# Low parts of the weights made by adding transfers instead of VectorE subtractions, in the first projection of a decoder trunk

## The chip, the cores and the metric

The kernel runs on one core of a Trainium2 chip. What is measured is the device time of one execution in microseconds. Engines are named as in the profile: PE is TensorE (matrix products; PEld its weight loads), DVE is VectorE, ACT is ScalarE, POOL is GpSimd, and SP is SyncE, which here only issues transfers.

## The reference

One recurrent layer (RG-LRU) is followed by one attention layer, on a sequence of 1024 positions with 1024 channels. The change lies in the first projection of the recurrent layer:

```python
h = rms_norm(x, norm_g)
u = h @ w_in                                  # 1024 x 1024 times 1024 x 2560
xb, gate = u[..., :D_RNN], u[..., D_RNN:]     # D_RNN = 1280
xb = causal_depthwise_conv(xb, conv_w, conv_b)
r = sigmoid(einsum(xblk, w_rg) + b_rg)        # 10 blocks of 128 channels
i = sigmoid(einsum(xblk, w_ig) + b_ig)
a = exp(log_a);  bterm = sqrt(-expm1(2 log_a)) * (i * xb)
y = scan(a, bterm) * silu(gate);  x = x + y @ w_out
```

## The kernel before

All arrays lie with channels on the 128 partitions and positions along the row. Products are made in a rounded 32-bit type (`F32R`) in three passes, to keep nearly the full precision of float32: each factor is split into a high part (rounded) and a low part (what the rounding left), and `mm3` (L116 to L119) adds high times high (L117), high times low (L118) and low times high (L119). The weight is the first factor, so L119 is the only one of the three that reads the low part of the weights, `wl`; L117 and L118 read the high part, `wh`.

Weights come in blocks of 128 rows by 512 columns (256 KB), two blocks for one output tile of 128 channels (`wtile`, `wload`). For each block, SP loads the raw values into `wr`. In the form used for most blocks of the first projection (`cast=True`), POOL's queue issues a second transfer of the same bytes that rounds them on the way into `wh` (L100), and VectorE subtracts `wh` from `wr` and writes `wl` (L101). The other form (`hl`, L85 and L86) rounds on ScalarE and subtracts on VectorE. There are two buffers for `wr`, four for `wh` and four for `wl`, so the blocks of two output tiles are held at once, and a buffer is written again when TensorE has read it for the last time.

The stage begins with column tile 0, whose weights come in the `hl` form while x is loaded and split. Its products run over eight pieces of x. Meanwhile the squares of x are summed in `accp`; the sum is split (`t`, L85 and L86), added over partitions by products with ones (L362), and turned into the norm's factor on ScalarE and VectorE (L142 to L145). The factor is applied to the products later, so those of tile 1 need not wait for it. Behind the ones-products TensorE goes on with the convolution branch of tile 1, whose two blocks are the first of the `cast` form; their low parts are `wl_327` and, in the order below, `wl_333` before and `wl_334` after.

Then a loop runs over ten column tiles. In each, TensorE makes 48 products of 128x512 for the gate half, 48 for the convolution half of the next tile and 12 for the two gates `r` and `i`. ScalarE and VectorE do the convolution (L382, L384), the sigmoids, the exponentials and roots, and the scan. The nine later gate blocks (`wgate`, 128 KB, one buffer) are of the `cast` form too. That makes 36 blocks of 256 KB and nine of 128 KB.

Each engine works through its own list in order. The lists come from a scheduler that goes by priorities and by its own estimates; the start of the stage, on SP, ScalarE and VectorE, is kept in the order in which it is written. POOL's queue is a list too: a transfer that waits holds up those behind it.

Of the kernel before, what the change touches and what calls it, by code (L numbers as in the profile page):

```python
# [11 lines left out]
AF = mybir.ActivationFunctionType  # L12
ALU = mybir.AluOpType
# [47 lines left out]
def trunk(tc, xT, wina, vecs, wgate, wouta, winc, wuk, wuv, wuq, wuqr, woutb, rope, outT):  # L61
    nc = tc.nc
    V, A, T, G = nc.vector, nc.scalar, nc.tensor, nc.gpsimd
# [10 lines left out]
    def nm(s):  # L74
        uid[0] += 1
        return f"{s}_{uid[0]}"
# [4 lines left out]
    def f(ap):  # L81
        return ap.bitcast(F32)

    def hl(src, hi, lo):
        A.activation(out=hi, in_=src, func=AF.Copy)  # L85
        V.tensor_tensor(out=lo, in0=src, in1=f(hi), op=ALU.subtract)  # L86

    def wload(src, n, gain=None, tag="w", pool=wp, rb=2, hb=4, pri=True, cast=False):

        with tc.high_priority(offset=WPRI if pri else 0):  # L90
            raw = pool.tile([P, n], F32, tag=tag + "r", bufs=rb, name=nm("wr"))
            hi = pool.tile([P, n], F32R, tag=tag + "h", bufs=hb, name=nm("wh"))
            lo = pool.tile([P, n], F32R, tag=tag + "l", bufs=hb, name=nm("wl"))
            nc.sync.dma_start(out=raw, in_=src)
            if gain is not None:
                k = n // P
                r3 = raw.rearrange("p (k m) -> p k m", m=P)
                V.tensor_tensor(out=r3, in0=r3, in1=gain.unsqueeze(2).to_broadcast([P, k, P]), op=ALU.mult)
            if cast:
                G.dma_start(out=hi, in_=src)  # L100
                V.tensor_tensor(out=lo, in0=raw, in1=f(hi), op=ALU.subtract)  # L101
            else:
                hl(raw, hi, lo)
        return hi, lo

    def wtile(src, nk, gain=None, step=4, cast=False, pri=True):

        ks = []
        for k0 in range(0, nk, step):
            k1 = min(nk, k0 + step)  # L110
            hi, lo = wload(src[:, k0 * P:k1 * P], (k1 - k0) * P, None if gain is None else gain[:, k0:k1], cast=cast, pri=pri)
            for k in range(k1 - k0):
                ks.append((hi[:, k * P:(k + 1) * P], lo[:, k * P:(k + 1) * P]))
        return ks
# [175 lines left out]
    with tc.manual_schedule(engines={_E.SP, _E.Activation, _E.DVE}):  # L290
# [60 lines left out]
        for k in range(done, NKT):  # L351
            squares(k)
        ws = wload(wgate[0], 2 * P, tag="s", pool=ta, rb=1, hb=1)
        wx = wtile(wina[1], NKT, cast=True)
        ap = [(tt(F32R), tt(F32R)) for _ in range(2)]
# [87 lines left out]
    for ct in range(NCT):  # L443
        ps = ps0[:2] if ct == 0 else psn
        pg1 = pg1 if ct == 1 else None
        if ct:
            ws = wload(wgate[ct], 2 * P, tag="s", pool=ta, rb=1, hb=1, cast=True)
        if 0 < ct < NCT - 1:
            wx = wtile(wina[ct + 1], NKT, cast=True)
        elif ct:  # L450
            wo = wtile(wouta[0], NCT)
        xcs = conv(ct, ps)
        gt = gates_a(ct, wg, (ps0[2:], pg1, None)[min(ct, 2)])
        if prev is not None:
            tail(*prev)
        if ct + 1 < NCT:
            wg = wtile(wina[NCT + ct + 1], NKT, cast=True)
            psn = [pst(), pst()]
            for h in range(2):
                mmt(psn[h], wx, xs, hs(h))  # L460
            if ct == 0:
                pg1 = [pst(), pst()]
                for h in range(PG1):
                    mmt(pg1[h], wg, xs, hs(h))
            prev = (ct, rgig(ct, ws, xcs), gt)
            if ct == 0:
                for h in range(PG1, 2):
                    mmt(pg1[h], wg, xs, hs(h))
# [129 lines left out]
    for k0, k1 in ((0, 4), (4, 6), (6, 10)):  # L598
        for i in range(2):
            hi, lo = wload(wouta[3 + 4 * i][:, k0 * P:k1 * P], (k1 - k0) * P)  # L600
# [595 lines left out]
```

## Time and profile before

| What | Value |
|---|---|
| median of three runs | 866.79 us (866.57 to 866.79) |
| span of the profiled execution, first to last instruction | 864.5 us |
| TensorE busy | 851.9 us (99%) |
| VectorE busy | 659.5 us (76%) |
| ScalarE busy | 519.9 us (60%) |
| POOL busy | 73.6 us (9%) |
| subtractions of the changed form (L101) | 45, from 28.4 to 244.1 us |
| table loads in ScalarE's list | 45 |
| mean granted TensorE clock | 0.996 |

Times in the profile run from the span's start. A row of the timeline gives start, length, engine, line, operation, `out<-in` and the count of instructions merged; in brackets stands the idle time before it and what ended that. A row of groups gives the count, the busy time with the mean of one in ns, and the idle time before. A row of transfers gives count, size and median time from issue to landing. Neighbouring instructions of one engine overlap a little, so starts are closer together than lengths.

### The profile page before, as it was taken

Reading aid. Unit: us, or ns where it says so; the run is one execution under the profiler, and the core shown is the slowest. Engines: PE = TensorE matmul, PEld = TensorE weight load, DVE = VectorE, ACT = ScalarE, POOL = GpSimd, SP = SyncE. Lnnn points to the kernel's source line nnn. Section 1 sums busy time; section 2 is a strip of 40 time slices with the busy share of each in tenths; the row PEclk is TensorE's granted clock in tenths of the full one; section 3 lists DMA queues with packets and bytes.
Section 4 is the critical chain, followed back from the end, with each engine's and each line's share of the span. In section 5 each row is a group of like instructions: output and inputs, shape, how many; then the busy total and the mean of one; then the engine's idle time right before and its main releaser. Section 6 shows DMA issues by size and latency. Waiting matters only on the chain.

```text
span 864.5 us, 11922 instructions
## 1 busy us (share of the span) xinstructions
PE 851.9 (99%) x4206; PEld 721.7 (83%) x4206; DVE 659.5 (76%) x1216; ACT 519.9 (60%) x959; POOL 73.6 (9%) x143
## 2 busy tenths in 40 slices
PE   8999999999999999999999999999999999999995
PEld 6788888888888888888888889888998998888885
DVE  7888778777877773779998957887797887875254
ACT  8557787777688542699976555555565564431132
POOL 1000110110000110100312320000000000010000
PEclk9999999999999999999999999999999999999998
DMA  8333333333213445123545674122231323867022
GB/s 300 92 98 98 98 97 99 107 95 98 79 43 92 151 144 184 51 98 121 170 147 202 213 252 125 53 91 83 77 113 62 105 82 132 335 211 247 0 98 98
DMA packets 51052, 108.98 MB, mean 126 GB/s; under 512 B 6448, under 2 KB 15024, under 8 KB 50992
## 3 DMA queue, kind: packets, MB, share of 16 engines
q1 hardware_dynamic: 34928, 67.05, 23.7%
q0 software_dynamic: 15216, 40.51, 14.1%
q8 instruction: 33, 0.54, 0.3%
q10 hardware_dynamic: 848, 0.66, 0.2%
q14 instruction: 27, 0.22, 0.1%
HBM read 81.46 MB, written 26.21 MB: 125 GB/s over the span
## 4 chain that ended last, share of the span: by engine, by line
PE 95%; DVE 2%; issue 1%; DMA 1%; ACT 1%; SPq 0%; DVEq 0%
PE ps L118 18%; PE ps L117 18%; PE ps L119 18%; PE pm L119 6%; PE pm L117 6%; PE pm L118 6%; PE pm L922 4%; PE pm L938 2%; PE pm L939 2%; PE s L905 2%; PE s L903 2%; PE s L904 2%; PE s L906 2%; PE s L902 2%; PE pm L937 2%
## 5 line engine op out<-in xcount | busy, mean ns | idle before, releaser
L118 PE MATMUL ps<-pg,wh 128*128 128x512 f32 x664 | 258.7, 390 | 0.6 <-DVE pg L256 0.5
L119 PE MATMUL ps<-pg,wl 128*128 128x512 f32 x664 | 258.4, 389 | 0.0
L117 PE MATMUL ps<-pg,wh 128*128 128x512 f32 x664 | 257.8, 389 | 0.0
L118 PEld LDWEIGHTS ps<-pg,wh 128*128 128x128 f32 x664 | 124.6, 188 | 27.7 <-DVE pg L256 2.1
L117 PEld LDWEIGHTS ps<-pg,wh 128*128 128x128 f32 x664 | 124.6, 188 | 26.3 <-DVE tk L657 0.3
L119 PEld LDWEIGHTS ps<-pg,wl 128*128 128x128 f32 x664 | 124.6, 188 | 25.7
L85 ACT ACTIVATE pt<-pm 128x512 fp32r<-128x512 f32 (+2 forms) x96 | 44.4, 490 | 58.1 <-PE pm L922 54.8
L912 ACT ACTIVATE pg<-s,m 128x128 f32<-128x128 f32 (+3 forms) x64 | 47.5, 743 | 47.1 <-DVE m L909 40.7
L117 PE MATMUL pm<-pg,pg 128*128 128x512 f32 (+1 forms) x152 | 54.9, 361 | 0.0
L118 PE MATMUL pm<-pg,pg 128*128 128x512 f32 (+1 forms) x152 | 54.5, 359 | 0.0
L119 PE MATMUL pm<-pg,pg 128*128 128x512 f32 (+1 forms) x152 | 54.3, 357 | 0.0
L86 DVE TENSOR_TENSOR pt<-pm,pt 128x512 fp32r<-128x512 f32 (+2 forms) x96 | 50.5, 549 | 3.2 <-ACT pt L85 3.2
L909 DVE TENSOR_REDUCE m<-s 128x1 f32<-128x128 f32 (+3 forms) x64 | 48.1, 753 | 1.2
L384 DVE SCALAR_TENSOR_TENSOR t<-xb,vec,t 128x512 f32<-128x512 f32 x60 | 44.8, 746 | 0.4
L85 ACT ACTIVATE wh<-wr 128x512 fp32r<-128x512 f32 (+3 forms) x55 | 29.1, 531 | 25.4 <-PE ps L118 12.9
L85 ACT ACTIVATE pg<-pg 128x512 fp32r<-128x512 f32 x42 | 26.1, 631 | 29.5 <-DVE pg L438 18.1
L86 DVE TENSOR_TENSOR wl<-wr,wh 128x512 fp32r<-128x512 f32 (+3 forms) x55 | 30.6, 566 | 15.5 <-ACT wh L85 15.3
L119 PE MATMUL pm<-pg,wl 128*128 128x512 f32 x108 | 42.4, 392 | 0.0
L922 PE MATMUL pm<-ident,pg 128*128 128x128 f32 x288 | 42.3, 274 | 0.0
L118 PE MATMUL pm<-pg,wh 128*128 128x512 f32 x108 | 42.3, 392 | 0.0
L117 PE MATMUL pm<-pg,wh 128*128 128x512 f32 x108 | 42.2, 390 | 0.0
L902 PE MATMUL s<-pg,pg 128*128 128x512 f32 (+2 forms) x96 | 37.0, 386 | 0.4 <-ACT pg L912 0.4
(238 smaller groups left out, 1782.1 us busy)
## 6 DMA issues: line engine op xcount, KB each, us to landing
wr<-wina SPq DMA_DIRECT2D x38, 256.0 KB, 2.8
wh<-wina POOLq DMA_DIRECT2D x36, 256.0 KB, 2.9
wa<-winc SPq DMA_DIRECT2D x24, 256.0 KB, 3.2
ysd<-pg POOLq DMA_DIRECT2D x12, 512.0 KB, 3.0
pg<-ysd SPq DMA_DIRECT2D x12, 512.0 KB, 10.6
wr<-wouta SPq DMA_DIRECT2D x16, 256.0 KB, 2.7
t<-xT SPq DMA_DIRECT2D x16, 256.0 KB, 3.6
x1d<-t POOLq DMA_DIRECT2D x16, 256.0 KB, 2.5
```

What stands on the lines that cost most here:

```text
L85: A.activation(out=hi, in_=src, func=AF.Copy)
L86: V.tensor_tensor(out=lo, in0=src, in1=f(hi), op=ALU.subtract)
L117: T.matmul(out=ps, lhsT=w[0], rhs=r[0], start=first, stop=False, skip_group_check=more)
L118: T.matmul(out=ps, lhsT=w[0], rhs=r[1], start=False, stop=False, skip_group_check=more)
L119: T.matmul(out=ps, lhsT=w[1], rhs=r[0], start=False, stop=last, skip_group_check=more)
L384: V.scalar_tensor_tensor(out=xc, in0=xb[:, j:j + HW], scalar=cwv[j], in1=xc, op0=ALU.mult, op1=ALU.add)
L902: T.matmul(out=sc[:, c], lhsT=q[0][:, ql], rhs=k[0][:, c], start=True, stop=False)
L903: T.matmul(out=sc[:, c], lhsT=q[0][:, ql], rhs=k[1][:, c], start=False, stop=False)
L904: T.matmul(out=sc[:, c], lhsT=q[1][:, ql], rhs=k[0][:, c], start=False, stop=False)
L909: V.tensor_reduce(out=m, in_=sc, axis=AX.X, op=ALU.max, negate=True)
L912: A.activation(out=p_[:, 0:nk], in_=sc, func=AF.Exp, bias=m, accum_out=l)
L922: T.transpose(out=ps[:, (b - b0) * P:(b - b0 + 1) * P], in_=p_[:, b * P:(b + 1) * P], identity=ident)
```

## The change

In the `cast` form, the subtraction on VectorE is replaced. ScalarE writes minus the raw block into `wl`, rounded as it is written; then a second transfer on POOL's queue reads the raw block from memory and adds it onto what lies in `wl`. What is left there is raw minus rounded, as before.

```diff
             if cast:
                 G.dma_start(out=hi, in_=src)
-                V.tensor_tensor(out=lo, in0=raw, in1=f(hi), op=ALU.subtract)
+                A.activation(out=lo, in_=raw, func=AF.Copy, scale=-1.0)
+                G.dma_start(out=lo, in_=src, accum_op=ALU.add)
             else:
                 hl(raw, hi, lo)
```

One line is added, so lines from 102 on have a number that is one higher in the changed kernel.

The lists of the engines change with it. ScalarE, at the end of the sum of squares (`accp`); before:

```order
L85 ACTIVATE wh_320<-wr_319 128x256 [waits DMAHW1_49]
L85 ACTIVATE t_337<-accp 128x512 [waits DVE_49]
L85 ACTIVATE t_339<-accp 128x512
L142 ACTIVATE t_345<-ps_347 128x512 [waits PE_49]
L143 ACTIVATE t_346<-t_345 128x512 [waits Activation_49]
```

and after:

```order
L85 ACTIVATE wh_320<-wr_319 128x256 [waits DMAHW1_49]
L101 ACTIVATE wl_327<-wr_325 128x512 [waits DMAHW2_49,PE_49]
L101 ACTIVATE wl_334<-wr_332 128x512 [waits DMAHW3_49,PE_49]
L85 ACTIVATE t_339<-accp 128x512 [waits DVE_49]
L85 ACTIVATE t_341<-accp 128x512
L143 ACTIVATE t_347<-ps_349 128x512 [waits PE_49]
L101 ACTIVATE wl_433<-wr_431 128x512 [waits DMAHW4_49]
L144 ACTIVATE t_348<-t_347 128x512 [waits Activation_49]
L101 ACTIVATE wl_440<-wr_438 128x512 [waits DMAHW5_49]
```

Two copies now stand ahead of the splitting of the sum, and two between the steps of the norm.

POOL's queue, from its first weight transfer on; before:

```order
L100 DMA wh_326<-wina 128x512 [waits DVE_49,PE_49]
L100 DMA wh_332<-wina 128x512 [waits DVE_49,PE_49]
L100 DMA wh_430<-wina 128x512 [waits DVE_49,PE_49]
L100 DMA wh_436<-wina 128x512 [waits DVE_49,PE_49]
L100 DMA wh_574<-wina 128x512 [waits DMASW0_49,DVE_49,PE_49]
```

and after:

```order
L100 DMA wh_326<-wina 128x512 [waits DVE_49,PE_49]
L100 DMA wh_333<-wina 128x512 [waits DVE_49,PE_49]
L100 DMA wh_432<-wina 128x512 [waits DVE_49,PE_49]
L102 DMA wl_327<-wina 128x512 [waits Activation_49]
L102 DMA wl_334<-wina 128x512 [waits Activation_49]
L100 DMA wh_439<-wina 128x512 [waits DVE_49,PE_49]
L102 DMA wl_433<-wina 128x512 [waits Activation_49]
```

The adding transfers of the first two blocks stand behind the rounding transfer of the third, and ahead of that of the fourth.

TensorE's list where tile 1 begins; before:

```order
L362 MATMUL ps_347<-t_338,onesr 128x512 [waits DVE_49]
L117 MATMUL ps_441<-pg_144,wh_326 128x512 [waits DMASW0_49]
L118 MATMUL ps_441<-pg_145,wh_326 128x512
L362 MATMUL ps_356<-t_340,onesr 128x512 [waits DVE_49]
L119 MATMUL ps_441<-pg_144,wl_327 128x512
L117 MATMUL ps_441<-pg_168,wh_326 128x512
```

and after:

```order
L363 MATMUL ps_349<-t_340,onesr 128x512 [waits DVE_49]
L118 MATMUL ps_445<-pg_144,wh_326 128x512 [waits DMASW0_49]
L119 MATMUL ps_445<-pg_145,wh_326 128x512
L363 MATMUL ps_358<-t_342,onesr 128x512 [waits DVE_49]
L118 MATMUL ps_446<-pg_144,wh_326 128x512 [waits PE_49]
L119 MATMUL ps_446<-pg_145,wh_326 128x512
L120 MATMUL ps_445<-pg_144,wl_327 128x512 [waits DMASW3_49]
```

Two products of the second half (`ps_446`) have moved ahead of the first product with a low part, which now waits for the adding transfer itself. In the rest of TensorE's list the order is as before.

## The prediction

> **What bounds the kernel now.** I read the busy time in stretches first, to see which engine fills the stage that is changed.
>
> ```profile
> core 0: us, PE busy (x) PEld busy (x) DVE busy (x) ACT busy (x) POOL busy (x), PEclk, DMA share, GB/s
> 20.00:44.00 24.00, 23.55 (x103) 18.92 (x102) 21.20 (x39) 13.58 (x18) 2.12 (x4) 1.00 0.34 98
> 142.00:166.00 24.00, 24.00 (x107) 19.89 (x106) 19.25 (x32) 17.56 (x25) 2.65 (x5) 1.00 0.32 95
> 500.00:864.00 364.00, 354.98 (x2021) 311.71 (x2019) 257.15 (x541) 166.48 (x361) 15.00 (x28) 0.99 0.37 127
> 30.00:32.00 2.00, 1.64 (x7) 1.38 (x8) 0.91 (x2) 1.08 (x2) 0.00 (x0) 1.00 0.84 278
> 32.00:34.00 2.00, 2.00 (x11) 1.65 (x10) 0.56 (x1) 1.27 (x3) 0.00 (x0) 1.00 0.77 238
> ```
>
> In the steady part of the first projection (142 to 166 us) TensorE is busy 24.00 of 24.00 us, while VectorE is busy 19.25 and ScalarE 17.56. So time taken off VectorE there is taken off an engine that TensorE does not wait for. Next, TensorE's waits:
>
> ```profile
> PE ps L288 <- DVE onesd L136: 1.1, 1, 1.1
> PE ps L325 <- ACT pg L255: 0.9, 1, 0.9
> PE ps L118 <- DVE pg L256: 0.5, 1, 0.5
> PE ps L362 <- DVE t L86: 0.5, 1, 0.5
> ```
>
> The last of these lies where the first weights made in the changed way are used; the three others come before it. So the whole stage offers under 1 us to win, and the question is what the change can make TensorE wait for.
>
> **The place: the first pair of blocks, 26 to 35 us.** TensorE, ScalarE, VectorE, then the queues:
>
> ```profile
> 28.92 0.39 PE L119 MATMUL ps<-pg,wl 128*128 128x512 f32 x1
> 29.14 0.76 PE L362 MATMUL ps<-t,onesr 128*128 128x512 f32 x2
> 30.36 0.50 PE L362 MATMUL ps<-t,onesr 128*128 128x512 f32 x1 [0.45 <-DVE t L86]
> 30.69 0.40 PE L117 MATMUL ps<-pg,wh 128*128 128x512 f32 x1
> 30.93 0.39 PE L118 MATMUL ps<-pg,wh 128*128 128x512 f32 x1
> 31.16 0.40 PE L362 MATMUL ps<-t,onesr 128*128 128x512 f32 x1
> 31.39 0.39 PE L119 MATMUL ps<-pg,wl 128*128 128x512 f32 x1
> ```
>
> ```profile
> 26.69 0.40 ACT L85 ACTIVATE wh<-wr 128x256 fp32r<-128x256 f32 x1
> 28.19 1.16 ACT L85 ACTIVATE t<-accp 128x512 fp32r<-128x512 f32 x2 [1.10 <-DVE accp L150]
> 28.41 1.29 DVE L101 TENSOR_TENSOR wl<-wr,wh 128x512 fp32r<-128x512 f32 x2
> 29.61 1.29 DVE L86 TENSOR_TENSOR t<-accp,t 128x512 fp32r<-128x512 f32 x2
> 28.02 0.53 POOL L100 DMA_DIRECT2D wh<-wina  x1 [9.40 <-PE ps L119]
> 29.38 0.53 POOL L100 DMA_DIRECT2D wh<-wina  x1 [0.83 <-PE ps L119]
> 29.12 6.81 SPq L94 DMA_DIRECT2D wr<-wina  x4
> ```
>
> Before, the low parts come from VectorE at 28.41 to 29.70 and TensorE first reads one at 31.39. That is 1.7 us of slack, where later blocks have over ten (rows below).
>
> **The change, part by part.** What goes and what comes, priced:
>
> ```profile
> L101 DVE TENSOR_TENSOR wl<-wr,wh 128x512 fp32r<-128x512 f32 x36 | 24.6, 686 | 7.2 <-DMA wh<-wina 4.4 <-DMA wr<-wina 2.7
> L85 ACT ACTIVATE wh<-wr 128x512 fp32r<-128x512 f32 x4 | 2.5, 623 | 0.2 <-PE ps L118 0.2
> L85 ACT ACTIVATE wh<-wr 128x256 fp32r<-128x256 f32 x3 | 1.2, 401 | 0.0
> L433 ACT ACT_TABLE_LOAD x9 | 11.5, 1283 | 0.2
> wh<-wina POOLq DMA_DIRECT2D x34, 256.0 KB, 2.9
> ```
>
> Removed: 36 subtractions on VectorE, 24.6 us, and nine of half width. Worth nothing on the path, because TensorE is full there.
>
> Added on ScalarE: 36 copies at 0.623 and nine at 0.401 = 26.0 us. The new order also has 53 table loads in place of 45, since copies pushed the two square roots of a block apart in four blocks: 8 at 1.283 = 10.3 us. Over nine blocks that is 4.0 us each on 17.56 us of 24. It is hidden by ScalarE's idle 6.4 us; in a block with the split roots it is 2.9 + 2.6 = 5.5 us, nearly all of it. If that cover goes, the third rival applies.
>
> Added on POOL's queue: 45 transfers, 36 of 256 KB. In the steady stage they are hidden by the distance from release to use:
>
> ```profile
> 126.39 0.53 POOL L100 DMA_DIRECT2D wh<-wina  x1 [7.63 <-PE ps L119]
> 142.47 0.39 PE L117 MATMUL ps<-pg,wh 128*128 128x512 f32 x1
> 133.85 0.69 DVE L86 TENSOR_TENSOR t<-t,t 128x512 fp32r<-128x512 f32 x1
> 141.11 0.39 PE L117 MATMUL ps<-t,wh 128*128 128x512 f32 x1
> ```
>
> A block's buffers are released at 126.39 and its weights used from 142.47: 16.1 us, for a copy (0.62) and a transfer of a few us. Behind a copy that waits for that release stand ScalarE's convolution roundings (L85), and TensorE waits for those at the gate products: VectorE ends them at 134.54, TensorE begins at 141.11, 6.6 us of room. So I cost the steady stage at nothing. That room is thinner once, in the first block:
>
> ```profile
> 42.07 0.53 POOL L100 DMA_DIRECT2D wh<-wina  x1 [2.19 <-PE ps L119]
> 47.40 0.69 DVE L86 TENSOR_TENSOR t<-t,t 128x512 fp32r<-128x512 f32 x1
> 48.86 0.39 PE L118 MATMUL ps<-t,wh 128*128 128x512 f32 x1
> ```
>
> The low part is done at 48.09 and read at 48.86. In the new order a copy that waits for the release at 42.07 stands ahead of that rounding, and behind the convolution's first step. Copy to 42.7, taps on VectorE to about 44.5, rounding to 45.1, low part to 45.8: 3 us of room, and a stall before it moves both ends alike.
>
> The start is different, and gives the sum. ScalarE is free at 27.09 and waits 1.10 us for the sum of squares. Two copies of about 0.6 us fill that gap, 27.1 to 28.25; the rounding behind them starts at most 0.1 us late. The first ends near 27.7. Its adding transfer cannot leave then. On POOL the rounding transfer of the third block stands ahead of it and waits for TensorE until 28.02.
>
> ```profile
> 357.86 1.22 POOL L499 DMA_DIRECT2D x1d<-t  x2 [20.54 <-DVE t L498]
> ```
>
> Two issues back to back take 1.22 us, so the next leaves 0.61 us later: 28.63.
>
> **Landing.** The trace has no adding transfer. From below: 2.9 us, the median of the rounding ones, so 31.5. From above: the slowest of this place,
>
> ```profile
> wh<-wina POOLq DMA_DIRECT2D x1, 256.0 KB, 5.2
> ```
>
> plus a second pass over its bytes (the old content is read too), 0.256 MB at 278 GB/s = 0.9 us: 6.1, so 34.7. That 5.2 is the transfer issued at 29.38, the last of four of 256 KB and one of 128 KB; they were through 6.6 us after the first issue at 28.02. In the new order the raw load of the third block goes out when the copy ends, near 27.7 (not at 29.12), and with the third block's rounding transfer, the next raw load and a gate block it is ahead of or beside the adding one: again four of 256 KB and one of 128. 27.7 + 6.6 = 34.3. I take that: the row from the same crowd is nearer than the median of a quiet stage.
>
> TensorE stands there meanwhile. In the new order it has done two more products (row to row 0.23 us, 0.45 together) than before at 31.39. Loss = 34.3 - 31.39 - 0.45 = +2.5 us. From the ends: 31.5 gives -0.3, 34.7 gives +2.9; were the weights there at once, +0 for them and -0.8 for the waits before the ones-products that two subtractions no longer cause.
>
> TensorE has no idle time later in which this could be made up. The span is 864.5 us and the median of the runs 866.79, so 2.3 us lie outside it and stay. 866.8 + 2.5 = **869.3 us**. The second block of the pair, 0.6 us behind, is needed 12 products (2.7 us) later and does not add. Behind the stall, the norm's chain on VectorE is sooner rather than later: before, it stood behind a subtraction that waited for a raw load,
>
> ```profile
> 33.44 0.69 DVE L101 TENSOR_TENSOR wl<-wr,wh 128x512 fp32r<-128x512 f32 x1 [2.54 <-DMA wr<-wina]
> ```
>
> and now the copies of that pair wait on ScalarE, between its norm steps, for loads that were issued 1.4 us sooner.
>
> **A rule against the trace.** The Trainium skill ("DMA: Bandwidth & Descriptors", Anatomy of one DMA) gives a transfer of this path about 2.0 us plus its bytes over 436 GB/s. By that estimate 256 KB take 2.6 us and the queue of 1.18 MB 4.7 us, so landing at 32.4 and a loss of 0.6 us. Going by that, the first rival below would be the result. The trace disagrees here: 278 and 238 GB/s, and 5.2 us for one.
>
> **The rivals.**
> - *The weights land nearly in time.* Landing between 2.9 and 4.8 us after the issue, as the quiet stage has it; the loss is -0.3 to +1.6, middle +0.8: 867.6. For it: queue order, since only one POOL transfer is ahead. Against it: the 5.2 us row. This is the case that ends on the other side: not slower by what can be told, and it decides as soon as the landing is under 4.8 us.
> - *Adding is much dearer than copying.* Twice the 5.2 us: 10.4, landing at 39.0, loss 7.2: 874.0. The steady stage still hides it (16.1 us). For it: each byte is read twice and added, and no row shows such a transfer. Against it: only that a factor of two is a guess at the far end. Before 500 us the granted clock is 1.00 in every stretch above, and TensorE's longest wait 1.1 us, so what a stall of 7 us does to the clock no row shows. The Trainium skill ("TensorE: Matmul & The Clock Gate", Part 1) says that an idle window of some 3.4 us halves the clock for about as long, which by estimate would be 1.7 us more.
> - *ScalarE becomes the bound.* In four blocks it has 17.56 + 5.5 = 23.1 us of work in some 24, and it waits for VectorE in between. If 2 us a block were lost there, the 6.6 us of room is gone after three blocks; the fourth would cost about 2 us: 871.2. For it: little idle time. Against it: VectorE loses 2.7 us a block itself, and those waits shrink.
> - *That the subtraction stays in some form* is excluded: VectorE's new order has no row of it.
>
> **How the numbers follow.** Forecast (869.3; own range 868.5 to 870.5) 0.46; in time 0.36; dear adding 0.12; ScalarE 0.06. About 0.2% (1.7 us) is what a measurement of this kernel can tell from no change. The forecast counts as slower, so do the last two; "in time" is the same; for faster by 1.7 us there is no idle time to win, 0.02. That gives slower 0.62, same 0.36. For 8 in 10 the range runs from 866.5 (the lower end of "in time") to 873.0 (half of the dear cases are left out).
>
> **What would show it.** Right: a TensorE wait of 2 to 4 us near 31 us, at the first product with a low part (L120 of the changed kernel), released by an adding transfer that landed 5 to 6 us after its issue near 28.6; no other new wait up to 500 us; VectorE's busy time down by about 28 us (24.6 and the nine of half width) and ScalarE's up by about 36. Wrong: that wait under 1 us, or a landing under 4 us (in time); a landing of 8 us or more (dear adding); TensorE waits at the gate products for ScalarE or VectorE (ScalarE). A TensorE clock under 1.00 after the wait would bear out the page on the clock.

## The result, and the profile after

The changed kernel takes 875.50 us (median of four runs, 874.22 to 876.08) against 866.79 (866.57 to 867.04) before: a ratio of 1.010, 95% interval 1.0086 to 1.0114. It is slower by 8.7 us, where 2.5 were forecast and the range ended at 873.0. The profiled execution is the longest of the four (876.08, span 874.3), so its gap to the span before is a little larger, 9.8 us. The working below is made against those 9.8.

Busy time in stretches, core 0 of the kernel after; the columns are those of the prediction's first fence:

```profile
20.00:44.00 24.00, 18.84 (x70) 14.67 (x69) 17.25 (x29) 13.64 (x19) 4.62 (x6) 0.86 0.54 129
44.00:265.00 221.00, 221.00 (x976) 182.99 (x975) 157.52 (x262) 187.31 (x264) 58.24 (x82) 1.00 0.58 134
380.00:500.00 120.00, 118.77 (x519) 96.81 (x518) 104.58 (x169) 98.45 (x224) 20.60 (x39) 1.00 0.46 155
```

The same stretches before:

```profile
44.00:265.00 221.00, 221.00 (x977) 183.00 (x976) 178.08 (x305) 163.49 (x223) 20.67 (x39) 1.00 0.31 90
380.00:500.00 120.00, 120.00 (x530) 99.11 (x529) 109.94 (x178) 95.61 (x213) 24.81 (x46) 1.00 0.47 160
```

In the long middle (44 to 265 us) TensorE is full before and after. Time is lost at the start, where the mean granted clock also falls to 0.86, and again after 380 us, a stage in which the change has no instruction. TensorE's waits after the change:

```profile
PE ps L120 <- DMA wl<-wina: 5.2, 1, 5.2
PE ps L118 <- ACT ps L638: 1.1, 2, 0.9
```

The first is the forecast wait for the first low part, 5.2 us where 2 to 4 were forecast. The second was not there before. Next the start, on TensorE and on POOL, which answer to the rows that the prediction shows of before:

```profile
30.74 0.39 PE L119 MATMUL ps<-pg,wh 128*128 128x512 f32 x1
36.29 0.79 PE L120 MATMUL ps<-pg,wl 128*128 128x512 f32 x1 [5.16 <-DMA wl<-wina]
36.89 0.63 PE L118 MATMUL ps<-pg,wh 128*128 128x512 f32 x1
37.31 0.63 PE L119 MATMUL ps<-pg,wh 128*128 128x512 f32 x1
...
42.01 0.57 PE L118 MATMUL ps<-pg,wh 128*128 128x512 f32 x1
42.41 0.39 PE L119 MATMUL ps<-pg,wh 128*128 128x512 f32 x1
42.65 0.40 PE L120 MATMUL ps<-pg,wl 128*128 128x512 f32 x1
```

```profile
27.86 0.53 POOL L100 DMA_DIRECT2D wh<-wina  x1 [9.39 <-PE ps L119]
28.39 1.82 POOL L102 DMA_DIRECT2D wl<-wina  x2
29.49 1.28 POOL L100 DMA_DIRECT2D wh<-wina  x1
```

The adding transfer was issued at 28.39 (forecast 28.63) and landed 7.9 us later, at 36.29 (forecast 5.6 and 34.3). After the wait TensorE's rows start 0.427 us apart where 0.227 is usual, up to 42.41. The granted clock was 0.50 from 35.55 to 42.38 us; this stretch is cut where the record of the clock changes:

```profile
35.55:42.38 6.83, 6.09 (x14) 4.79 (x15) 5.65 (x16) 3.20 (x4) 0.58 (x1) 0.50 0.77 189
```

So the 9.8 us divide as follows.

- *The wait.* Without it the product at 36.29 would have started at 31.84 (31.39 and 0.45, as in the prediction): 4.45 us.
- *The slow clock.* From 36.29 to 42.41 there are 14 starts in 6.12 us; at 0.227 they are 3.18: 2.9 us.
- *The rest*, 2.4 us, is lost after 380 us. TensorE's products can be counted off against those of before: the same product starts 7.5 us later at 380 us and 9.8 us later from 430 us on. The largest step, before and after:

```profile
427.22 0.39 PE L117 MATMUL ps<-pg,wh 128*128 128x512 f32 x1
436.92 0.50 PE L118 MATMUL ps<-pg,wh 128*128 128x512 f32 x1 [0.92 <-ACT ps L638]
```

### The profile page after: what moved, and what is told of

It reads as the page before. It is cut to its first block, busy times and chain, and to the rows that moved or that the text cites. A ratio compares the mean times of both kernels' runs of the same rounds, so it can differ in the third digit from the quotient of the medians.

```text
span 874.3 us, 12008 instructions
## 1 busy us (share of the span) xinstructions
PE 856.0 (98%) x4206; PEld 723.9 (83%) x4206; DVE 639.1 (73%) x1171; ACT 551.5 (63%) x1012; POOL 113.7 (13%) x188
## 4 chain that ended last, share of the span: by engine, by line
PE 90%; ACT 3%; DMA 2%; DVE 2%; issue 1%; POOL 0%; SPq 0%; DVEq 0%; POOLq 0%; ACTq 0%
PE ps L120 16%; PE ps L118 16%; PE ps L119 16%; PE pm L120 6%; PE pm L119 6%; PE pm L118 6%; PE pm L923 4%; PE pm L939 2%; PE pm L940 2%; PE s L906 2%; PE s L904 2%; PE s L905 2%; PE s L907 2%; PE s L903 2%; PE pm L938 2%
## 5 line engine op out<-in xcount | busy, mean ns | idle before, releaser
L119 PEld LDWEIGHTS ps<-pg,wh 128*128 128x128 f32 x664 | 125.4, 189 | 27.7 <-DVE pg L257 1.6
L100 POOL DMA_DIRECT2D wh<-wina x36 | 24.0, 667 | 117.7 <-PE ps L120 108.3
```

The source lines that it names most:

```text
L119: T.matmul(out=ps, lhsT=w[0], rhs=r[1], start=False, stop=False, skip_group_check=more)
```

## The experiments

The kernel before was run beside each, on the same chip: 866.6 us for the first four experiments, 866.9 for the others. Ratios are to those runs.

**1. The first pair of blocks alone keeps the subtraction.**

```diff
-                A.activation(out=lo, in_=raw, func=AF.Copy, scale=-1.0)
-                G.dma_start(out=lo, in_=src, accum_op=ALU.add)
+                if cast == "sub":
+                    V.tensor_tensor(out=lo, in0=raw, in1=f(hi), op=ALU.subtract)
+                else:
+                    A.activation(out=lo, in_=raw, func=AF.Copy, scale=-1.0)
+                    G.dma_start(out=lo, in_=src, accum_op=ALU.add)
...
-        wx = wtile(wina[1], NKT, cast=True)
+        wx = wtile(wina[1], NKT, cast="sub")
```

> The first two blocks of the changed form (for column tile 1) get their low parts by VectorE's subtraction again; the other 34 blocks and the nine gate blocks keep ScalarE's copy and the adding transfer. Theory (the loss is a stall of 4.5 us at the first pair, 2.6 us of slow clock behind it, and some 2.2 us near 380 to 440 us that have another cause, the place of a buffer, which is the same in this kernel): the first two terms go, 875.5 - 7.1 = 868.4, no TensorE wait near 31 us, clock 1.00. Rival (the adding transfers and ScalarE's copies slow the whole stage down): only a ninth part of them is gone, so 873 or more.

Measured: 869.98 us, ratio 1.0039 (1.0025 to 1.0053). The wait and the slow clock are gone; from 44 to 265 us TensorE is busy 221.00 of 221.00. That is 5.5 us less, and refutes the rival, but 3.4 us stay where the theory had room for less. They lie after 380 us, by the stretch and by TensorE's waits:

```profile
380.00:500.00 120.00, 118.07 (x516) 96.18 (x515) 108.35 (x175) 95.33 (x216) 23.10 (x43) 1.00 0.48 161
```

```profile
PE ps L121 <- ACT ps L641: 0.9, 2, 0.7
PE ps L121 <- DVE tk L661: 0.9, 1, 0.9
```

Counted off as above, the products are 0.2 us late at 380 us and 3.4 from 445 us on. So the later stage loses 3.2 us here and 2.4 in the changed kernel, which has no wait like the second of these, at 445 us: the two losses don't simply add.

**2. TensorE kept busy ahead of the wait.** One product of tile 1 is made twenty times more, into a bank that is written anew afterwards, just before tile 1's products. That changes nothing in what TensorE waits for, only how long it is idle.

```diff
         if ct + 1 < NCT:
...
             psn = [pst(), pst()]
+            if ct == 0:
+                for _ in range(20):
+                    T.matmul(out=psn[1], lhsT=wx[0][0], rhs=xs[0][0][:, hs(1)], start=True, stop=True)
```

> Twenty products that repeat the first one of the second half (their result is overwritten, nothing is left out) stand ahead of the first product that needs a low part, 4.5 us of work in the 5.2 us in which TensorE waited. Theory (the half clock follows from TensorE standing still for over 5 us): the wait shrinks to under 1 us, the granted clock stays 1.00, the 13 products behind go at 0.227 us and not at 0.427, and the time falls by 2.6 us to 872.9. Rival (the slow products have to do with the transfers that land at that time, not with the wait): they stay slow, 875.5.

Measured: 872.84 us, ratio 1.0072 (1.0057 to 1.0087). The low part is again there only at 35.93, and TensorE does twenty products more, yet the kernel is 2.7 us shorter than the changed one:

```profile
35.93 0.50 PE L120 MATMUL ps<-pg,wl 128*128 128x512 f32 x1 [0.44 <-DMA wl<-wina]
36.27 0.39 PE L118 MATMUL ps<-pg,wh 128*128 128x512 f32 x1
36.50 0.40 PE L119 MATMUL ps<-pg,wh 128*128 128x512 f32 x1
```

With 0.44 us of idle time instead of 5.16, the rows behind it start 0.23 us apart. The slow rows were a consequence of the idle time. By TensorE's rows the start is 2.8 us shorter than in the changed kernel, which is what the account gives: 2.9 for the slow rows and 0.4 for the earlier landing, less 0.45 for two products that stand behind the first low part here and ahead of it there.

**3. The second transfer without adding.** It writes the raw block, rounded, over the copy: the low parts hold the rounded weights, and the subtraction is left out.

```diff
-                G.dma_start(out=lo, in_=src, accum_op=ALU.add)
+                G.dma_start(out=lo, in_=src)
```

> The second transfer of a block writes the rounded block over ScalarE's copy and doesn't add; this leaves out the subtraction, so the low parts hold the rounded weights themselves. Queue, order, waits and bytes from memory stay as they are. Theory of the prediction (the landing is set by the crowd of transfers, the adding costs at most a second pass of 0.9 us): the first one lands 7 us or more after its issue, the time stays within 1 us of 875.5. Rival (adding is dear in itself): it lands after 5.5 us, TensorE waits some 2.7 us, the clock does not fall, and the time is 875.5 - 2.4 - 2.6 = 870.5.

Measured: 872.57 us, ratio 1.0067 (1.0052 to 1.0082). The start on POOL and TensorE, and the transfers issued between 29.0 and 29.9 us:

```profile
29.14 1.07 POOL L102 DMA_DIRECT2D wl<-wina  x2
```

```profile
35.02 0.51 PE L120 MATMUL ps<-pg,wl 128*128 128x512 f32 x1 [3.12 <-DMA wl<-wina]
35.37 0.40 PE L118 MATMUL ps<-pg,wh 128*128 128x512 f32 x1
```

```profile
wl<-wina POOLq DMA_DIRECT2D x2, 256.0 KB, 5.9
```

A plain transfer in the same place and the same crowd lands 5.9 us after its issue, close to the 5.6 of the forecast. So the crowd gives the 5.6 to 5.9, and what the adding one needs beyond it belongs to the adding. The time itself missed both expectations: 870.5 held no account of what is lost after 380 us, and this run loses that too (118.74 of 120 us busy there). Adding transfers of the first block landed after 7.9 us in the changed kernel, and after 7.3, 6.8 and 6.6 in experiments 2, 4 and 7 (start of the first product with a low part, less the issue: 35.93 - 28.67, 36.09 - 29.32, 35.41 - 28.83): 0.7 to 2.0 us for the adding. Each is one profile, so how much of the spread is the crowd's is not shown. The quiet stage shows it without the spread. Transfers issued from 60 to 240 us, after the change and here:

```profile
wh<-wina POOLq DMA_DIRECT2D x30, 256.0 KB, 3.4
wl<-wina POOLq DMA_DIRECT2D x30, 256.0 KB, 5.8
```

```profile
wl<-wina POOLq DMA_DIRECT2D x30, 256.0 KB, 3.9
wh<-wina POOLq DMA_DIRECT2D x28, 256.0 KB, 3.2
```

The adding transfer of the same bytes takes 1.9 us more. The wait here was 3.1 us, and the clock stayed at 1.00.

**4. Other places for the first output weights.** What is lost after 380 us needed a cause. The loads of the weights `winc` into the buffers `wa` start late after the change; the queue of SP before, after, and in experiment 1:

```profile
369.18 24.20 SPq L529 DMA_DIRECT2D wa<-winc  x11
```

```profile
381.41 16.32 SPq L530 DMA_DIRECT2D wa<-winc  x9
```

```profile
374.16 21.22 SPq L533 DMA_DIRECT2D wa<-winc  x11
```

After the change the start is 12.2 us later than before, though the program is only 7.5 late at that point. `wa` lies where tiles of the finished stage lay, and waits until they are done with. The compiled programs give the addresses: the first `wa` begins at 214240 in both. The tile `t` with the block a22, which `wpair` splits last, is at 202976 before, but at 215264 after, under `wa`. The temporaries `t` form a ring, and in the reordered first projection they are handed out in another order, so everything later in the ring moves. Here three writes of one column each take three places of the ring ahead of these blocks; nothing else in the kernel is changed.

```diff
+    V.memset(tt()[:, 0:1], 0.0)
+    V.memset(tt()[:, 0:1], 0.0)
+    V.memset(tt()[:, 0:1], 0.0)
     w0 = wpair(0, tt)
```

> Three of the stage's 512-column buffers are taken out of turn, each with one column set to zero, ahead of the first weight blocks of the joint projection, so that those blocks get other places in the ring; nothing is left out. Theory (the last 2.2 us come from the seven weight loads that in the changed kernel could start only at 381.4 us, because the first of them goes into memory under a block that is split until then, and in the kernel before started at 369.2): the loads start some 4 us sooner, TensorE's wait for L638 (1.1 us) is gone, 875.5 - 2.2 = 873.3. Rival (ScalarE or VectorE is behind there because of the changed stage): no change, 875.5.

Measured: 873.15 us, ratio 1.0073 (1.0058 to 1.0088), 2.35 us faster than the changed kernel. The loads start at 376.69, and from 380 to 500 us TensorE is busy 119.39 us in place of 118.77. The start was shorter in this run as well (a wait of 4.0 us; slow rows for 3.1 us, from 36.09 to 39.17), so the 2.35 us are not the place's alone. Counted off against before, the products are 5.8 us late at 380 us and 7.0 at 500, in place of 7.5 and 9.8: the stage loses 1.2 us where it lost 2.4. The next experiment tries the place with the start out of the way.

**5. Both: the first pair subtracts, and the three writes.**

> The first pair of blocks keeps the subtraction on VectorE, and three one-column writes ahead of the first output weights give these other places in the ring of temporaries; the other 43 blocks add. Theory (the stall with its slow clock, and the buffer place, are the whole loss; the 43 adding blocks of the steady stage cost nothing): the loads of `wa` from `winc` start before 378 us, TensorE is busy over 119.4 of 120 us from 380 to 500 us, and the time is that of before: 866.3 to 867.6. Rival (the 3.4 us left when only the first pair was undone come from the 43 adding blocks themselves, from the load on POOL's queue and ScalarE): 869 to 870.5, as then.

Measured: 868.29 us, ratio 1.0017 (1.0008 to 1.0026): 1.7 us under experiment 1, and 1.4 above before. Neither expectation holds. Up to 380 us hardly anything is lost (114.97 us busy of 115 from 265 us on), the loads of `wa` start at 371.51, and still TensorE is busy 118.67 of 120 us. ScalarE shows a second wait of the same kind; its first `cc` copy before, after, and here:

```profile
372.27 0.58 ACT L637 ACTIVATE cc<-ps 128x512 f32<-128x512 f32 x1
```

```profile
380.82 0.60 ACT L638 ACTIVATE cc<-ps 128x512 f32<-128x512 f32 x1 [0.99 <-DVE acc L153]
```

```profile
373.33 0.60 ACT L644 ACTIVATE cc<-ps 128x512 f32<-128x512 f32 x1 [0.38 <-DVE acc L156]
```

`cc` begins at 208096, and a square of the last residual tiles lies under it, at 207072. It is the second of the four that VectorE adds up before the change, the fourth after it, and the third here; the copy waits until it is added. From there ScalarE's copies run 1.1 us later than before (the third `cc` at 410.52 for 409.42), and TensorE waits 0.4 us for ScalarE at 428 us. Its larger wait, 0.9 us at 444 us, comes another way: TensorE waits for VectorE, VectorE for ScalarE, and ScalarE for a transfer out of a tile `tk`. Experiment 1 has this wait too (1.11 us); before and after the change it is not there.

```profile
439.11 0.63 ACT L147 ACTIVATE tk<-tk 128x512 f32<-128x512 f32 x1 [1.14 <-DMA kvd<-tk]
439.77 0.69 DVE L148 SCALAR_TENSOR_TENSOR tk<-ps,tk 128x512 f32<-128x512 f32 x1 [0.99 <-ACT tk L147]
444.12 0.50 PE L121 MATMUL ps<-pg,wh 128*128 128x512 f32 x1 [0.92 <-DVE tk L664]
```

**6. The kernel before, with the first pair's subtractions behind the splitting of the sum.**

```diff
+    late = []
...
-                V.tensor_tensor(out=lo, in0=raw, in1=f(hi), op=ALU.subtract)
+                if cast == "late":
+                    late.append((lo, raw, hi))
+                else:
+                    V.tensor_tensor(out=lo, in0=raw, in1=f(hi), op=ALU.subtract)
...
-        wx = wtile(wina[1], NKT, cast=True)
+        wx = wtile(wina[1], NKT, cast="late")
...
             hl(accp[:, hs(h)], *ap[h])
+        for lo, raw, hi in late:
+            V.tensor_tensor(out=lo, in0=raw, in1=f(hi), op=ALU.subtract)
```

> The kernel before, with one thing moved: the two subtractions of the first pair stand behind the splitting of the sum of squares on VectorE, so that the ones-products of the norm need not wait for them. Theory: the wait of 0.45 us at the ones-products goes, and the low parts, two subtractions later (about 31.0 us), are still there when read at about 31: 866.2, a gain of 0.3 to 0.5 us, near the limit of what can be told. Rival: the first low part is now late by 0.3 to 0.6 us, so the wait only moves: 866.6 to 866.9.

Measured: 866.31 us, ratio 0.9994 (0.9985 to 1.0003). TensorE's stretch at the start is full now, where it was 23.55:

```profile
20.00:44.00 24.00, 24.00 (x107) 19.40 (x106) 23.37 (x44) 14.22 (x19) 2.11 (x4) 1.00 0.35 104
```

The wait of 0.45 us went and did not come back elsewhere in it. The interval holds 1, so the gain is shown in the profile and not in the time. The stretch has no more idle time to give.

**7. Only the first pair adds; the other 43 blocks subtract.** The edit is that of experiment 1 with the branches exchanged.

> Only the first pair of blocks adds; the other 43 keep the subtraction. The places of the first output weights are those of before. Theory: the start alone makes a wait of 4 to 5.2 us with a half clock behind it, 6.5 to 7.2 us in all: 873 to 874, and from 44 to 500 us TensorE loses nothing against before. Rival (the first adding transfer is late because those of the third and fourth block crowd it): with them gone it lands 6 us after its issue, the wait is about 3 us, the clock stays at 1.00, and the time is 869 to 870.

Measured: 873.22 us, ratio 1.0077 (1.0063 to 1.0091). The rival expected at most 870 and falls.

```profile
35.41 0.80 PE L123 MATMUL ps<-pg,wl 128*128 128x512 f32 x1 [3.81 <-DMA wl<-wina]
36.00 0.63 PE L121 MATMUL ps<-pg,wh 128*128 128x512 f32 x1
...
40.69 0.55 PE L123 MATMUL ps<-pg,wl 128*128 128x512 f32 x1
41.08 0.39 PE L121 MATMUL ps<-pg,wh 128*128 128x512 f32 x1
```

```profile
380.00:500.00 120.00, 120.00 (x530) 98.99 (x529) 106.62 (x172) 97.93 (x224) 22.02 (x41) 1.00 0.46 153
```

Two transfers of 45 make 6.3 us: 3.6 for the wait (35.41 less 31.84) and 2.7 for the slow rows (13 starts in 5.67 us, where 2.95 are usual). With the places of before (this program has the same addresses), nothing is lost from 380 to 500 us.

**8. The first pair subtracts, and the places are chosen.** Five writes ahead of the first output weights and two ahead of the squares, so that the square under `cc` is again the second. The first pair is as in experiment 1.

```diff
+    V.memset(tt()[:, 0:1], 0.0)
...
     w0 = wpair(0, tt)
     factors(3, *x1s)
+    V.memset(tt()[:, 0:1], 0.0)
+    V.memset(tt()[:, 0:1], 0.0)
     for i in range(4):
         sq_a(i % 2, x1s[i])
```

> The first pair of blocks keeps the subtraction and the other 43 blocks add, as in the run with pair and buffer, but the one-column writes into the ring of temporaries are seven, five ahead of the first output weights and two ahead of the squares of the last residual tiles. So the tile that lies under the first `wa` is free early, and the tile that lies under the first `cc` is that of the second square and not of the third or fourth, as before. Theory (both waits are matters of place, and the 43 adding blocks cost nothing themselves): ScalarE's first `cc` copy waits for no sum of squares, TensorE is busy over 119.8 of 120 us from 380 to 500 us, and the time is 866.3 to 867.2, that of before. Rival (the 1.4 us left there come from the 43 adding blocks): 868.0 to 868.6 again.

Measured: 867.32 us, ratio 1.0005 (0.9996 to 1.0014): not to be told from before, 0.1 us above the theory's figure and well under the rival's.

```profile
373.89 0.58 ACT L648 ACTIVATE cc<-ps 128x512 f32<-128x512 f32 x1
```

```profile
44.00:265.00 221.00, 221.00 (x977) 183.00 (x976) 159.05 (x262) 191.39 (x269) 56.25 (x79) 1.00 0.60 133
380.00:500.00 120.00, 119.80 (x528) 98.36 (x526) 110.11 (x179) 96.51 (x217) 23.90 (x45) 1.00 0.47 158
```

The edit of experiment 1 and seven one-column writes: the writes are worth 869.98 - 867.32 = 2.7 us (2.9 by the ratios, each to its own run of before). Places are not all that moves with them. VectorE adds up one square, splits a block and then adds up the other three (at 371.14 and 372.98 us), where it adds up four in a row in experiment 5 (at 371.41). The first `cc` copy comes 0.56 us later than there, though it no longer waits, and ScalarE's wait for the transfer out of `tk` is 0.41 us in place of 1.14. So the loss after 380 us goes with the places of the later temporaries and the order of the lists together. What each of these waits is worth is not shown, and the copy's wait alone can't be the cost.

The adding form in the other 43 blocks costs nothing that can be told: the interval ends at 0.14%, 1.2 us, and of the 0.9 us by which the profiled span is longer than before, 0.7 lie after 380 us. It brings nothing either: VectorE is busy 19 us less from 44 to 265 us than before, and TensorE is as full there as it was.

## Why the prediction was wrong

The direction and the first place were right, the size was not. In the profiled run the 9.8 us are the forecast's 2.5, another 2.0 because the first low part landed at 36.29 and not at 34.3, 2.9 for the slow clock, which the sum did not have, and 2.4 after 380 us, where it had nothing. Undone singly, the start is worth 6.3 us (experiment 7) and the later stage 2.7 (experiments 1 and 8), together 9.0 for the 8.7 of the medians; the start differs from run to run, and the two parts don't simply add.

- *TensorE is full, so VectorE's relief is worth nothing:* right (experiment 8). VectorE's busy time fell by 20.4 us, not 28; ScalarE's rose by 31.6, not 36. The durations that I added up overlap their neighbours (two subtractions of 0.69 take 1.29), which explains a part.
- *The steady stage hides the 43 later blocks:* right, with 221.00 of 221.00 us. The rival that ScalarE becomes the bound falls with it, and the first block's 3 us of room sufficed.
- *The issue of the first adding transfer at 28.63:* right, 28.39. Each adding issue holds POOL some 0.85 us and not the 0.53 to 0.61 I used, so the transfers behind the first left later than I had reckoned.
- *The landing, 5.6 us after the issue:* this term of the sum failed first. "27.7 + 6.6 = 34.3" prices the crowd, and rightly: the plain transfer of experiment 3 lands after 5.9. It left out the adding, although the upper bound had named a second pass over the bytes at 0.9 us and so ended at 34.7. The adding cost 1.9 us in the quiet stage and up to 2.0 here; the landing was 36.29. The rival "adding is much dearer" had the mechanism, with 10.4 us for a transfer that took 7.9. That its 874.0 comes near the measured 875.5 is luck: its landing was 2.7 us too late, and it had nothing after 380 us.
- *The loss is the wait alone:* wrong by 2.9 us, the slow clock of the changed kernel. It stood only in that rival, in one sentence on the Trainium skill ("TensorE: Matmul & The Clock Gate", Part 1), for a wait of 7 us at 0.12. The sum put it at nothing, though no row showed what a wait of 2 to 4 us does to the clock. Here 3.1 us of idle time (experiment 3) left it at 1.00, and 3.8, 4.0 and 5.2 (experiments 7 and 4, the changed kernel) did not. By the lengths of the waits the trace agrees with the idle window of some 3.4 us that this page of the Trainium skill gives.
- *"No other new wait up to 500 us":* wrong. I followed the change through the stages that contain it. That the order of the first stage also decides where later temporaries lie, and with it what the next stage's buffers wait for and in what order its lists run, was in no step and no rival. The runs show that this loss goes without a change to the 43 later adding blocks (experiment 8); its division over the single waits stays open. It is 2.4 of the 9.8 us of the profiled run.
- *"In time":* falls, since no first adding transfer landed in under 6.5 us and the case needed under 4.8.

## What to carry to other kernels

A transfer that is hidden in the steady part of a loop can still stand at the front of TensorE's queue the first time round, so price the first iteration by itself, and add the clock's slowing where the wait comes near the 2.6 to 4.4 us after which the clock fell here; undoing the change for that first iteration alone took off 5.5 us here. A change that reorders tiles in a shared ring can move waits into a stage it doesn't touch: compare the addresses, the order of the lists and the first waits of the later stage before calling it unchanged. Relief for an engine is worth only what the bounding engine waits for it, which was under 1 us here; in the profile, experiment 6 removed 0.45 of it with two instructions moved.

## What was not expected of the hardware

- An adding transfer of 256 KB occupied POOL for 0.85 us at its issue, a rounding one before the change for 0.53, and it landed 1.9 us later than a plain one in the same place of a quiet stage (5.8 against 3.9).
- The half clock began before the wait was over, and lasted 6.83 us in the changed kernel, 6.82 in experiment 7 and 3.41 in experiment 4, after waits of 5.2, 3.8 and 4.0: one length or twice that length, and not in the order of the waits. Experiments 7 and 4, cut where the granted clock changes:

```profile
34.19:41.01 6.82, 5.60 (x13) 4.50 (x14) 5.50 (x15) 1.56 (x2) 0.00 (x0) 0.50 0.55 154
35.66:39.07 3.41, 2.98 (x7) 2.41 (x8) 2.80 (x8) 3.19 (x4) 0.57 (x1) 0.50 1.12 290
```

- The clock fell 4.4, 2.6 and 3.6 us after TensorE had gone idle (changed kernel, experiments 7 and 4), and did not fall in the 3.1 us of experiment 3. So the length of the wait alone doesn't decide. The Trainium skill says in the same section ("TensorE: Matmul & The Clock Gate", Part 1) that the window is free-running, so its position against the wait would differ from run to run. These runs are consistent with that, but none varied the position by itself.
